# Spreading the modulation steps of a hybrid GLA/Fourier diffusion layer: one per half unit, two at a head's middle output; a load on another queue

## The chip, the cores and the metric

The kernel runs on one core of a Trainium2 chip. The metric is the device time of one execution in microseconds (us). A core has five engines, each with its own instruction stream: TensorE (PE, matmuls; its weight loads are shown as PEld), VectorE (DVE), ScalarE (ACT), GpSimd (POOL) and SyncE (SP), which in this kernel only issues transfers (DMAs). ACT and POOL issue a few DMAs too. PE, DVE, ACT and POOL run in an order that the kernel's code gives; for SP's DMAs a scheduler chooses the order.

## The reference

One layer of a diffusion backbone on 128 context and 256 latent tokens, model width 2048, everything in float32. Cut to what matters here:

```python
def layer(x, cond, s0_f, s0_b, n_chunks, lw):
    mod = jax.nn.silu(cond) @ lw['w_ada'] + lw['b_ada']
    sh1, sc1, ga1, sh2, sc2, ga2 = [m[:, None, :] for m in jnp.split(mod, N_MOD, axis=-1)]
    h = rmsnorm(x, lw['norm_pre_mix']) * (1.0 + sc1) + sh1
    m, s_f, s_b = mixer(h, s0_f, s0_b, n_chunks, lw)
    x = x + ga1 * rmsnorm(m, lw['norm_post_mix'])
    h = rmsnorm(x, lw['norm_pre_ffn']) * (1.0 + sc2) + sh2
    ff = (jax.nn.silu(h @ lw['w_ffn_gate']) * (h @ lw['w_ffn_up'])) @ lw['w_ffn_down']
    return x + ga2 * rmsnorm(ff, lw['norm_post_ffn']), s_f, s_b

def mixer(h, s0_f, s0_b, n_chunks, lw):
    # h @ w_in: GLA q, k (4 heads x 128), v, output gate g (4 x 256), two decay factors (16 each),
    # Fourier groups (4 x 256)
    # branch A: gated linear attention in both directions, chunks of 64, RMSNorm per head, times silu(g)
    # branch B: real part of the 2-D DFT over positions and group channels
    gates = jax.nn.sigmoid(h @ lw['w_gate'] + lw['b_gate'])
    g_a, g_b = jnp.split(gates, 2, axis=-1)
    merged = g_a * (o @ lw['w_br_gla']) + g_b * (f @ lw['w_br_four'])
    return merged @ lw['w_out'], s_f, s_b
```

The modulation `cond @ w_ada` has two rows only (context and latent), but its weights are 2048 x 12288.

## The kernel before, in words

**Products.** Every matrix product is done in split float32: weights and inputs each have a high and a low part, and three matmuls (high-high, high-low, low-high) stand for one. A weight block of 128 x 1024 (512 KB) takes this path: SP loads it into `raw` (two buffers, and in some stages spare ones), ACT casts the high part `whi` (`split`; L301, or L292 and L295 for folded blocks), DVE subtracts the low part `wlo` (L288), PE multiplies (L327 in `gemm`). Four pairs `whi`/`wlo` exist; `push` splits one block each time a product takes one.

**Half units.** The stages until the output projection are made of units. `proj` does a unit of 128 output columns as two half units of 24 matmuls each; after each it calls `step(side)`, which lets side work go on by one step. Side work is written as Python generators, so a `yield` is the place where the work is cut, and the order of the instructions on each engine is that in which the generators are run.

**Stages in order.** Input norm and the v projection (to 142 us); the stage of GLA, with units for q and k and the gates 0 to 24, beside which `gla()` computes the four heads (to 442 us); the gates 25 to 31, beside which `run_after` prepares the Fourier branch (`ends`, `over_parts`: sums and differences of rows, L727 to L741; `across_n`: products L1040 and L1041 with weights that `fold_across` folds, L257 and L258; to 548 us); the units of GLA's output gate, o0 to o7, with `four` units between them (products L1240 and L1241; their weights are folded by L244 and L245, cast by L295; to 663 us); the branch-a units; `w_out`; and the feed-forward net, which takes the rest.

**The modulation.** The last four of the six vectors are computed beside all this. `ada_rest` goes through blocks; each has 16 granules. A granule loads 512 KB of `w_ada` from POOL's queue into `adaw` (two buffers). On DVE it multiplies and adds this into `adacc` (two instructions L708, one for each row; L706 for the first granule of a block). With `on_pe` set it goes to TensorE instead: four products L698, which are eight rows in a trace, into `pr`. After the granules come one empty step, then the row sums (L719, products with `selr`) and ACT's copy `adev` (L668), then in the next step two transposes L672 and DVE's L677. `ada` is `ada_gen` behind `paced`, which runs `rate[0]` steps for each call on average.

**GLA.** For each head: transposes and decay (`la`, ACT L819 to L821; split into `lah` and `lal`, L379 and L380), then for both directions the sums along the chunk (`bT`, L835), `qi` and `ki` (L851, L852), the scores (`at`, L875), states, and three outputs `po` (L789) for t = 0, 1, 2. A gate's unit ends with ACT's `gz` (L983) and a store of it (L984, issued by ACT). At the end DVE scales all outputs with the norms `rs` (L946).

**The end of GLA.** `low_later` makes `split` hold back the low part of a block until the next `split`, so that DVE does other work before it.

**The constants** `cd` for the Fourier branch (128 x 1934, L1063) are loaded in `run_after`, at its turn 7 of 14.

Of the kernel before, what the change touches and what calls it, by code (L numbers as in the profile page):

```python
# [37 lines left out]
XU = 2  # L38
GF = 25
GD = 256  # L40
TAIL = {1: True, 4: False, 5: True, 8: True, 10: False, 11: True, 14: False}
RATE = 1.07


C_TRI = 0
# [7 lines left out]
C_CE = C_SEL3 + 96  # L53
# [3 lines left out]
NC = C_CT + 2 * (HT + HL)  # L57
# [51 lines left out]
def tile_step(ctx: ExitStack, tc: tile.TileContext, a, o):  # L109
# [139 lines left out]
    low_later = [False]  # L249
# [434 lines left out]
    on_pe = [False]  # L684
# [69 lines left out]
    with ExitStack() as s:  # L754
# [25 lines left out]
        def gla():  # L780
# [10 lines left out]
            for h in range(NH):  # L791
# [34 lines left out]
                yield  # L826
                if h == 0:
                    yield
                for d in range(2):


                    bT = pss.tile([P, T], F32, tag="side", name="bT")
                    for t in range(3):
                        for j, l in enumerate((lah, lal)):
                            PE.matmul(  # L835
                                bT[:, t * P : (t + 1) * P], l[:, t, d], tri[:, d * P : (d + 1) * P],
                                start=j == 0, stop=j == 1,
                            )
                    sx = pss.tile([P, 2, P], F32, tag="side", name="sx")
                    for j, l in enumerate((lah, lal)):  # L840
                        PE.matmul(
                            sx, tri[:, (2 + d) * P : (3 + d) * P], l[:, 0 : 2 + d : 1 + d, d], start=j == 0, stop=j == 1,
                        )
                    eb = pg.tile([P, T], F32, tag=f"eb{d}", name="eb")
                    ACT.activation(eb, bT, AF.Exp)
                    ki = pg.tile([P, T], F32, tag=f"ki{d}", name="ki")
                    ACT.activation(ki, bT, AF.Exp, scale=-1.0)
                    ko = pg.tile([P, 2, P], F32, tag=f"ko{d}", name="ko")
                    ACT.activation(ko, sx, AF.Exp)
                    qi = pg.tile([P, T], F32, tag=f"qi{d}", name="qi")  # L850
                    DVE.scalar_tensor_tensor(qi, eb, DK**-0.5, qT[:, h, :], op0=ALU.mult, op1=ALU.mult)  # L851
                    DVE.tensor_mul(ki, ki, kT[:, h, :])  # L852
                    DVE.tensor_mul(ko, ko, krs[:, 0 : 2 + d : 1 + d, :])

                    last = 0 if d else CH - 1
                    tot = chunks(eb)[:, :, d, last : last + 1]
                    kc = pg.tile([P, 3, CH], F32, tag=f"kc{d}", name="kc")
                    DVE.tensor_mul(kc, chunks(ki)[:, :, d, :], tot.to_broadcast([P, 3, CH]))
                    dc = pg.tile([P, 1], F32, tag=f"dc{d}", name="dc")
                    c = 5 if d else 2  # L860
                    e0, e1 = c * CH + last, (c + 1 - 2 * d) * CH + last
                    DVE.tensor_mul(dc, eb[:, e0 : e0 + 1], eb[:, e1 : e1 + 1])
                    qin.append(qi)
                    kin.append(ki)
                    kcr.append(kc)
                    kout.append(ko)
                    dec.append((tot, dc))
                    yield
# [60 lines left out]
                for t in range(3):  # L929
                    po = pss.tile([P, DV], F32, tag="side", name="po")  # L930
                    mm3(po, [x[:, t, :] for x in ap], vh[t], True, t == 0)
                    if t:
                        for d in range(2):
                            st = (sp if t == 1 + d else S)[d]
                            mm3(po, [x[:, t, :] for x in qp[d]], [x[:, 0, :] for x in st], False, d == 1)
                    ACT.copy(on(t, h), po.rearrange("p (a b) -> p a b", a=2))
                    junk = pg.tile([P, DV], F32, tag="krs", name="junk")
                    ACT.activation(junk, po, AF.Square, accum_out=ss[:, t, h : h + 1])
                    yield
            rs = pg.tile([P, 3, 4], F32, name="rs")  # L940
            ACT.activation(rs, ss, AF.Sqrt, bias=eps_t[:, 0:1], scale=1.0 / DV)
            DVE.reciprocal(rs, rs)
# [25 lines left out]
        gl = gla()  # L968
        def side():
            while True:  # L970
                next(gl, None)
                next(ada, None)
                yield

        sd = side()
        rate[0] = RATE
        for i in qk_order[1:]:
            proj(psm, hT, keep(qk, i), sd)

# [36 lines left out]
    with ExitStack() as s:  # L1016
        more = s.enter_context(tc.tile_pool(name="more", bufs=1))
        hF = [actp.tile([P, 4, 2, T], F32R, tag=t, name="hF") for t in ("C_lo", "B_hi", "B_lo")]
        hF.append(more.tile([P, 4, 2, T], F32R, tag="hF", name="hF"))
        sums, folds = [], {}  # L1020

        def ends(n):
            t, r = (more.tile([P, 2, T], F32, tag=z, name=z) for z in ("t", "r"))
            over_ends(2 * n, t, r)
            over_parts(2 * n, r, False)
            folds[n] = r

        def across_n(h, n):
            if n == 0:
                sums[:] = [pss.tile([P, 2, hi - lo], F32, tag="side", name="pfo") for _ in range(2) for lo, hi, _ in parts]  # L1030
            w = take()
            push()
            w_of = [x.rearrange("p (g i k c) -> p i k g c", g=2, i=2, k=2) for x in w]
            for k in range(2):
                kt = 2 * n + k
                x = hF[kt // 4][:, kt % 4]
                for g in range(2):
                    for i, (lo, hi, _) in enumerate(parts):
                        p = sums[2 * g + i]
                        PE.matmul(p, w_of[0][:, i, k, g, :], x[:, :, lo:hi], start=kt == 0, stop=False)  # L1040
                        PE.matmul(p[:, 0], w_of[1][:, i, k, g, :], x[:, 0, lo:hi], start=False, stop=kt == KT - 1)  # L1041
            if n == 7:
                for g in range(2):
                    X.append(px.tile([P, T], F32, tag="yb", name="X", bufs=4))
                    for i, (lo, hi, _) in enumerate(parts):
                        p = sums[2 * g + i]
                        ACT.copy(X[-1][:, lo:hi], p[:, 1])
                        DVE.tensor_add(X[-1][:, lo:hi], X[-1][:, lo:hi], p[:, 0])

        def run_after():  # L1050
            for at, todo in enumerate(after):
                for what, *n in todo:
                    if what == "ends":
                        ends(*n)
                    elif what == "parts":
                        over_parts(2 * n[0], folds.pop(n[0]), True)
                    else:
                        if n == [1, 5]:
                            depth[0] = 2
                            spare_raws.clear()  # L1060
                        across_n(*n)
                if at == turns // 2:
                    SP.dma_start(cd, a["consts"][:, C_CE:NC])  # L1063
                if at in (turns - 4, turns - 3, turns - 1):
                    next(ada_gen, None)
                yield

        ra = run_after()
        low_later[0] = True
        for i in range(GF, 32):  # L1070
            proj(psm, hT, gate(more, i), ra)
            if i == GF:
                depth[0] = 4
                spare_raws.extend([lambda: more.tile([P, G], F32, tag="raw3", name="raw3", bufs=2)] * 2)
        catch_up()
        low_later[0] = False
        depth[0] = 0
        xq = px.tile([P, HT], F32, name="xq")
        POOL.memset(xq, 0.0)
        qb = pss.tile([P, HT], F32, tag="side", name="pfq")  # L1080
        for kb in range(0, KT, 4):
            for x_ in range(2):
                for k in range(kb, kb + 4):
                    q = 32 * (k % 4)
                    PE.matmul(
                        qb[q : q + 4, :], wq[:, k, :], hF[k // 4][:, k % 4, x_, 0:HT].bitcast(F32),
                        start=kb == 0 and x_ == 0, stop=kb == KT - 4 and x_ == 1,
                    )
        for q in range(0, P, 32):
            ACT.copy(xq[q : q + 4, :], qb[q : q + 4, :])  # L1090
# [3 lines left out]
    with ExitStack() as s:  # L1094
# [84 lines left out]

        def side():  # L1180
            while True:
                on_pe[0] = turn[0] > 5
                if turn[0] < 6 or turn[0] % 2:
                    next(ada_gen, None)
                on_pe[0] = False
                turn[0] += 1
                next(df, None)
                next(nw, None)
                yield
# [910 lines left out]
```

## Time and profile before

| what | value |
|---|---|
| median of 3 runs | 1955.28 us (1954.93 to 1955.28) |
| the profiled execution | 1954.75 us |
| its span | 1953.0 us |
| TensorE's clock granted, mean | 0.997 |
| PE busy | 1923.8 us |
| DVE busy | 1650.9 us |
| ACT busy | 915.7 us |
| POOL busy | 85.8 us |
| DMA packets | 200615, 380.52 MB |

The span is the time between the first and the last event of the profiled execution; the time of the execution itself has 1.75 us more around it. Busy times leave out waits and issuing. In a row of the timeline stand the start in us from the span's start, the duration, the engine and the line, the operation with the written tile and the ones read, the shape, how many such instructions stand together (x), and in brackets how long the engine was idle just before and what it waited for. In a row of windows stand for each engine its busy time and number of instructions, then TensorE's clock, the DMA engines' share and GB/s.

### The profile page before, as it was taken

How to read it: one execution, taken by the hardware profiler on the slowest of the kernel's cores; microseconds unless marked ns; L12 is line 12 of the kernel's file. 1: busy time of each engine (PE TensorE's matmuls, PEld its weight loads, DVE VectorE, ACT ScalarE, POOL GpSimd, SP SyncE). 2: the span in 40 equal slices, each digit the busy share in tenths (PEclk: the TensorE clock that was granted, in tenths of full speed). 3: DMA queues.
4: the chain of work that ended last, by engine and by line, in shares of the span. 5: the costliest groups of instructions: out<-in, count | busy, mean ns of one | idle time of the engine just before them, and what ended most of it. 6: DMA issues, size and time to landing. Idle time of an engine off the chain costs nothing.

```text
span 1953.0 us, 27535 instructions
## 1 busy us (share of the span) xinstructions
PE 1923.8 (99%) x10526; PEld 1692.8 (87%) x10526; DVE 1650.9 (85%) x2174; ACT 915.7 (47%) x1298; POOL 85.8 (4%) x154
## 2 busy tenths in 40 slices
PE   8999999999999999999999999999999999999997
PEld 5779999999999999999988888888888888888876
DVE  5668898989868897987789898999998999888885
ACT  4235445544455644456454444444444444444444
POOL 0001111110000000004000000000000000000001
PEclk9999999999999999999999999999999999999999
DMA  9977766766556895656254635363636263625243
GB/s 390 387 257 240 252 223 230 261 233 219 181 161 227 297 310 190 222 195 220 81 176 148 189 109 190 126 207 110 205 109 215 93 221 92 200 76 183 86 168 112
DMA packets 200615, 380.52 MB, mean 195 GB/s; under 512 B 14196, under 2 KB 126932, under 8 KB 196132
## 3 DMA queue, kind: packets, MB, share of 16 engines
q1 hardware_dynamic: 181396, 321.83, 48.7%
q0 software_dynamic: 13952, 50.39, 8.5%
q10 hardware_dynamic: 5136, 6.56, 0.9%
q8 instruction: 82, 1.34, 0.3%
q14 instruction: 49, 0.40, 0.1%
HBM read 361.94 MB, written 16.78 MB: 194 GB/s over the span
## 4 chain that ended last, share of the span: by engine, by line
PE 71%; DVE 3%; DMA 1%; ACT 1%; issue 0%; ACTq 0%; DVEq 0%; SPq 0%
PE pgu L339 30%; PE pdn L339 18%; PE pmm L327 17%; PE pf L1240 1%; PE pmm L1517 1%; PE pfo L1040 1%; PE ptr L1809 1%; PE pf L1241 1%; DMA raw<-in_w_d 0%; DMA raw<-in_w_gate 0%; PE pfo L1041 0%; DVE adacc L708 0%; DVE x1b L1961 0%; DMA raw<-in_w_in 0%; PE pr L698 0%
## 5 line engine op out<-in xcount | busy, mean ns | idle before, releaser
L327 PE MATMUL pmm<-A_hi,wlo 128*128 128x384 f32 x1072 | 360.0, 336 | 4.2 <-DVE wlo L288 4.2
L327 PE MATMUL pmm<-A_hi,whi 128*128 128x384 f32 x1072 | 362.8, 338 | 0.0
L327 PE MATMUL pmm<-A_lo,whi 128*128 128x384 f32 x1072 | 359.6, 335 | 0.0
L1664 ACT CAST whi<-u 128x1024 fp32r<-128x1024 f32 x200 | 210.6, 1053 | 281.6 <-DVE u L1648 86.2
L1664 ACT CAST whi<-raw 128x1024 fp32r<-128x1024 f32 x175 | 184.2, 1052 | 202.0 <-PE pgu L339 59.4
L1675 DVE TENSOR_TENSOR wlo<-u,whi 128x1024 fp32r<-128x1024 f32 x200 | 244.3, 1222 | 31.5 <-ACT whi L1664 17.9
L339 PE MATMUL pgu<-whi,A_hi 128*128 128x512 f32 x640 | 250.0, 391 | 0.0
L339 PE MATMUL pgu<-whi,A_lo 128*128 128x512 f32 x640 | 249.3, 389 | 0.0
L1675 DVE TENSOR_TENSOR wlo<-raw,whi 128x1024 fp32r<-128x1024 f32 x175 | 213.7, 1221 | 38.5 <-ACT whi L1664 30.8
L288 DVE TENSOR_TENSOR wlo<-raw,whi 128x1024 fp32r<-128x1024 f32 x163 | 198.3, 1220 | 25.8 <-ACT whi L301 24.4
L301 ACT CAST whi<-raw 128x1024 fp32r<-128x1024 f32 x149 | 155.9, 1050 | 120.8 <-PE pmm L327 57.2
L327 PEld LDWEIGHTS pmm<-A_hi,wlo 128*128 128x128 f32 x1072 | 202.1, 188 | 4.9 <-DVE wlo L288 4.9
L327 PEld LDWEIGHTS pmm<-A_hi,whi 128*128 128x128 f32 x1072 | 202.1, 188 | 3.4 <-issue 2.5
L708 DVE SCALAR_TENSOR_TENSOR adacc<-adaw,spad,adacc 128x1024 f32<-128x1024 f32 x162 | 200.6, 1280 | 2.4 <-DMA adaw<-in_w_ada 1.9
L327 PEld LDWEIGHTS pmm<-A_lo,whi 128*128 128x128 f32 x1072 | 202.2, 189 | 0.2
L339 PE MATMUL pdn<-whi,hid_hi 128*128 128x512 f32 x480 | 186.9, 389 | 0.0
L339 PE MATMUL pdn<-whi,hid_lo 128*128 128x512 f32 x480 | 186.8, 389 | 0.0
L339 PE MATMUL pgu<-wlo,A_hi 128*128 128x512 f32 x640 | 184.2, 389 | 0.0
L339 PEld LDWEIGHTS pgu<-whi,A_hi 128*128 128x128 f32 x640 | 120.2, 188 | 26.1 <-issue 0.8
L339 PEld LDWEIGHTS pgu<-wlo,A_hi 128*128 128x128 f32 x640 | 120.1, 188 | 25.4
L339 PEld LDWEIGHTS pgu<-whi,A_lo 128*128 128x128 f32 x640 | 120.1, 188 | 25.0
L339 PE MATMUL pgu<-whi,S 128*128 128x512 f32 x480 | 131.1, 395 | 0.0
(405 smaller groups left out, 3042.7 us busy)
## 6 DMA issues: line engine op xcount, KB each, us to landing
adaw<-in_w_ada POOLq DMA_DIRECT2D x96, 512.0 KB, 3.9
raw<-in_w_d SPq DMA_DIRECT2D x88, 512.0 KB, 3.7
slab<-in_w_ada SPq DMA_DIRECT2D x32, 1024.0 KB, 10.0
raw<-in_w_gate SPq DMA_DIRECT2D x64, 512.0 KB, 4.6
raw<-in_w_g SPq DMA_DIRECT2D x48, 512.0 KB, 3.5
raw<-in_w_u SPq DMA_DIRECT2D x48, 512.0 KB, 3.6
raw<-in_w_in SPq DMA_DIRECT2D x44, 512.0 KB, 4.2
u<-in_w_u SPq DMA_DIRECT2D x40, 512.0 KB, 4.7
```

Source lines behind the costliest of these rows:

```text
L288: eng.tensor_sub(lo, raw, hi.bitcast(F32))
L301: ACT.copy(hi, raw)
L327: PE.matmul(dst, w[wi][:, k * n + n0 : k * n + n0 + P], x[xi][:, k0 + k, :], start=first and k == 0 and j == 0, stop=last and k == kts - 1 ...
L339: PE.matmul(dst, stat[x_][m], mov(w[w_], m), start=first and w_ == m == x_ == 0, stop=last and w_ == m == 1,)
L708: DVE.scalar_tensor_tensor(acc[:, c, :], w, spad[:, k, c : c + 1], acc[:, c, :], op0=ALU.mult, op1=ALU.add,)
L1040: PE.matmul(p, w_of[0][:, i, k, g, :], x[:, :, lo:hi], start=kt == 0, stop=False)
L1240: PE.matmul(pf[:, 0 : 2 * HT], w[0][:, c], x[k], start=k == 0, stop=False)
L1241: PE.matmul(pf[:, 0:HT], w[1][:, c], x[k][:, 0:HT], start=False, stop=m == 1 and k == 3)
L1517: PE.matmul(hp[u], hw[u][j][:, ((k - 1) % 8) * P : ((k - 1) % 8 + 1) * P], h2[m][:, k - 1, :], start=k == 1 and j == m == 0, stop=k == KT ...
L1664: ACT.copy(hi, src)
L1675: DVE.tensor_sub(lo, src, hi.bitcast(F32))
L1809: PE.transpose(pt[:, j, :], src[:, j * P : (j + 1) * P], ident)
```

## The change

Six edits, all but one of the order:

1. `TAIL` names the branch-a units that do a modulation granule, `True` for TensorE. It had 1, 5, 8 and 11 on TensorE, and 4, 10 and 14 on DVE; it has 8 on TensorE, and 4, 10, 13 and 15 on DVE.
2. In the GLA stage `side` drives `ada_gen` itself: once in each half unit, and twice in the one of a head's middle output (`yield t == 1`). The pace of 1.07 steps for each half unit goes.
3. Head 0 has one more `yield` between its decay and the sums along the chunk.
4. `cd` is loaded from ACT's queue and not from SP's.
5. `low_later` is set after the first of the gate units 25 to 31 and not ahead of it.
6. In the o units the half units 0 to 6 and 8 have their granule on DVE, and 7, 9, 11, 13 and 15 on TensorE; before, DVE had 0 to 5 and TensorE 7, 9, 11, 13 and 15.

```diff
-TAIL = {1: True, 4: False, 5: True, 8: True, 10: False, 11: True, 14: False}
-RATE = 1.07
+TAIL = {4: False, 8: True, 10: False, 13: False, 15: False}
...
                 split_act(lah, lal, la)
                 yield
                 if h == 0:
+                    yield
                     yield
                 for d in range(2):
...
                     ACT.activation(junk, po, AF.Square, accum_out=ss[:, t, h : h + 1])
-                    yield
+                    yield t == 1
...
         gl = gla()
         def side():
             while True:
-                next(gl, None)
-                next(ada, None)
+                light = next(gl, None)
+                for _ in range(2 if light else 1):
+                    next(ada_gen, None)
                 yield
 
         sd = side()
-        rate[0] = RATE
...
                 if at == turns // 2:
-                    SP.dma_start(cd, a["consts"][:, C_CE:NC])
+                    ACT.dma_start(cd, a["consts"][:, C_CE:NC])
...
         ra = run_after()
-        low_later[0] = True
         for i in range(GF, 32):
             proj(psm, hT, gate(more, i), ra)
             if i == GF:
                 depth[0] = 4
+                low_later[0] = True
...
         def side():
             while True:
-                on_pe[0] = turn[0] > 5
-                if turn[0] < 6 or turn[0] % 2:
+                on_pe[0] = turn[0] > 6 and turn[0] != 8
+                if turn[0] < 9 or turn[0] % 2:
                     next(ada_gen, None)
```

In the rows that follow, lines of the changed kernel are one lower than those of the same code before, up to about L826.

DVE's order at the first `four` unit inside o3, before and after. `ws` is the folded Fourier weight block, `adacc` and `adaw` are the modulation's sums and weights, `fd` takes the product.

```order
L244 TENSOR_TENSOR ws<-raw_5909 128x512
L245 TENSOR_TENSOR ws<-raw_5909 128x512
L288 TENSOR_TENSOR wlo<-ws,whi 128x1024
L288 TENSOR_TENSOR wlo<-raw_5911,whi 128x1024
L1245 TENSOR_TENSOR fd<-fd,pf 128x194 x2
```

After the change, the same place:

```order
L243 TENSOR_TENSOR ws<-raw_5909 128x512
L244 TENSOR_TENSOR ws<-raw_5909 128x512
L707 SCALAR_TENSOR_TENSOR adacc<-adaw,spad,adacc 128x1024 x2
L287 TENSOR_TENSOR wlo<-ws,whi 128x1024
L287 TENSOR_TENSOR wlo<-raw_5911,whi 128x1024
L1245 TENSOR_TENSOR fd<-fd,pf 128x194 x2
```

A granule has come between the fold and the low part; the same happens in o4.

DVE's order where the GLA stage ends and `run_after` begins, before. `qk` holds the heads' outputs, `rs` their norms; `t`, `r` and `hF` are the sums of rows; `raw` is a weight block as loaded.

```order
L946 TENSOR_SCALAR qk<-qk,rs 128x2x128 x4
L727 TENSOR_TENSOR t<-A_hi,A_lo 128x768
L732 TENSOR_TENSOR r<-t 128x2x64
L733 TENSOR_TENSOR r<-t 128x2x63
L732 TENSOR_TENSOR r<-t 128x2x128
L733 TENSOR_TENSOR r<-t 128x2x127
L257 TENSOR_TENSOR raw<-raw 128x2x256
L258 SCALAR_TENSOR_TENSOR raw<-raw 128x2x256
L288 TENSOR_TENSOR wlo<-raw,whi 128x1024
L739 TENSOR_TENSOR hF<-r,hF 128x2x384
```

After the change, the same place:

```order
L946 TENSOR_SCALAR qk<-qk,rs 128x2x128 x8
L287 TENSOR_TENSOR wlo<-raw,whi 128x1024
L726 TENSOR_TENSOR t<-A_hi,A_lo 128x768
L731 TENSOR_TENSOR r<-t 128x2x64
L732 TENSOR_TENSOR r<-t 128x2x63
L731 TENSOR_TENSOR r<-t 128x2x128
L732 TENSOR_TENSOR r<-t 128x2x127
L256 TENSOR_TENSOR raw<-raw 128x2x256
L257 SCALAR_TENSOR_TENSOR raw<-raw 128x2x256
L738 TENSOR_TENSOR hF<-r,hF 128x2x384
```

The low part has moved from behind the fold (L257 and L258 before) to ahead of the sums of rows; eight scalings stand in a row where there were four.

PE's order in gate unit 2, before, at head 0's middle output (`po`; `pr` takes the row sums, `ptm` their transposes).

```order
L789 MATMUL po<-vr,ap 128x256 x3
L789 MATMUL po<-part,qp 128x256 x6
L719 MATMUL pr<-adacc,selr 32x256 x8
L327 MATMUL pmm<-A_hi,whi 128x384
```

After the change, at the same output, which comes one half unit later:

```order
L788 MATMUL po<-vr,ap 128x256 x3
L788 MATMUL po<-part,qp 128x256 x6
L718 MATMUL pr<-adacc,selr 32x256 x8
L671 MATMUL ptm<-ident,adev 128x128 x2
L326 MATMUL pmm<-A_hi,whi 128x384
```

The transposes, which stood a half unit behind the row sums, now follow them at once.

SP's order at the end of the GLA stage, before.

```order
L235 DMA raw_4617<-in_w_in 128x4x256
L235 DMA raw_4619<-in_w_gate 128x1024
L1063 DMA cd<-in_consts 128x1934
L235 DMA raw<-in_w_gate 128x1024
```

After the change:

```order
L234 DMA raw_4617<-in_w_in 128x4x256
L234 DMA raw<-in_w_gate 128x1024
L234 DMA raw_4619<-in_w_gate 128x1024
```

The load into the ordinary buffer now comes ahead of the one into the spare buffer, and `cd` is gone from SP; ACT issues it right behind the L740 of `run_after`'s turn 7.

## The prediction, made before the change was run

> **What bounds the kernel now.** I read the busy times and the chain that ended last first, then the list of what TensorE (PE) waited for.
>
> ```profile
> PE 1923.8 (99%) x10526; PEld 1692.8 (87%) x10526; DVE 1650.9 (85%) x2174; ACT 915.7 (47%) x1298; POOL 85.8 (4%) x154
> PE 71%; DVE 3%; DMA 1%; ACT 1%; issue 0%; ACTq 0%; DVEq 0%; SPq 0%
> PE pmm L327 <- DVE wlo L288: 4.2, 2, 3.7
> PE at L875 <- DVE ki L852: 1.8, 1, 1.8
> PE pr L719 <- DVE adacc L708: 1.5, 2, 0.9
> PE bT L835 <- DVE lal L380: 0.9, 2, 0.6
> ```
>
> The first row is busy us, share of the span and instructions; the second the chain by engine; the others what PE waited for: total us, how often, the longest. PE is busy 99% of the span, so an edit pays in two ways only: it takes work off PE, or removes one of PE's few waits. It costs where a VectorE (DVE) step comes late for PE. The four waits listed lie in the stages that the diff touches: 8.4 us in all.
>
> **Granules taken off TensorE.** By the order of instructions three fewer modulation granules (not four) are on PE: those of branch-a units 1, 5 and 11. Their price is seen at the one that PE ran at 689 us (start, duration, what):
>
> ```profile
> 688.85 0.33 PE L327 MATMUL pmm<-o_lo,whi 128*128 128x384 f32 x1
> 689.02 0.34 PE L327 MATMUL pmm<-o_hi,wlo 128*128 128x384 f32 x1
> 689.29 0.64 PE L698 MATMUL pr<-adaw,spad 128*32 128x256 f32 x8
> 689.86 0.45 PE L327 MATMUL pmm<-o_hi,whi 128*128 128x384 f32 x1
> ```
>
> From one product matmul to the next it is 689.02 − 688.85 = 0.17 us; across the granule 0.84. So a granule costs PE 0.67 us, and three cost **−2.0**. The list shows no PE wait in the branch-a units, so this comes off the end. The three come back on DVE: one in the branch-a units, two in the o units.
>
> **Two granules more on VectorE in the o units.** The order puts them at the first half unit of o3 and of o4, between the fold of the Fourier weights (L245) and their low part (L288), for which the product L1241 on PE waits.
>
> ```profile
> L708 DVE SCALAR_TENSOR_TENSOR adacc<-adaw,spad,adacc 128x1024 f32<-128x1024 f32 x162 | 200.6, 1280 | 2.4 <-DMA adaw<-in_w_ada 1.9
> 601.23 1.23 DVE L288 TENSOR_TENSOR wlo<-ws,whi 128x1024 fp32r<-128x1024 f32 x1 [1.12 <-ACT whi L295]
> 607.83 0.56 DVE L380 TENSOR_TENSOR o_lo<-gs,o_hi 128x384 fp32r<-128x384 f32 x1 [0.58 <-ACT o_hi L379]
> 608.78 1.22 DVE L288 TENSOR_TENSOR wlo<-ws,whi 128x1024 fp32r<-128x1024 f32 x1 [0.39 <-ACT whi L295]
> 603.64 0.25 PE L1241 MATMUL pf<-edT,wlo 128*128 128x194 f32 x1
> 610.23 0.25 PE L1241 MATMUL pf<-edT,wlo 128*128 128x194 f32 x1
> ```
>
> The low part that ends at 602.46 is used at 603.64: 1.18 to spare. The next ends at 610.00 and is used at 610.23: 0.23 to spare. A granule is two instructions of the first row; a pair takes 2.48 (row of 185.02 below), and 187.41 − 185.02 = 2.39 until the next instruction starts. In its place DVE now idles 1.12 for an ACT cast, so each new granule delays DVE by 1.27 net. The idles of 0.58 and 0.39 don't win that back: both end on ACT casts that follow on DVE's own work. Two delays less the 0.23 to spare make 2.3; I take **+2.2**, a little less for what ACT may catch up. Bounds: 2 × 2.39 = 4.8 if the idle isn't used, 0.5 if most of the delay is taken up by later idles. I stay near the middle, as it rests on rows of the very place.
>
> The one DVE granule more in the branch-a units I put at nothing: the weights there come through the same L288, on which PE doesn't wait in that stage; without that cover it would cost 2.4.
>
> **Start of the gate units 25 to 31.** Here lies PE's longest wait in these stages.
>
> ```profile
> raw<-in_w_gate SPq DMA_DIRECT2D x64, 512.0 KB, 4.6
> 443.99 1.06 ACT L301 CAST whi<-raw 128x1024 fp32r<-128x1024 f32 x1 [0.45 <-DVE wlo L288]
> 448.31 0.96 DVE L727 TENSOR_TENSOR t<-A_hi,A_lo 128x768 f32<-128x768 f32 x1
> 449.32 1.57 SPq L1063 DMA_DIRECT2D cd<-in_consts  x1
> 451.71 1.22 DVE L288 TENSOR_TENSOR wlo<-raw,whi 128x1024 fp32r<-128x1024 f32 x1
> 453.00 0.33 SPq L235 DMA_DIRECT2D raw<-in_w_gate  x1
> 452.00:456.50 4.50, 4.50 (x28) 4.50 (x27) 4.47 (x8) 1.69 (x3) 1.31 (x3) 1.00 1.02 344
> 455.95 0.84 ACT L741 CAST hF<-r 128x768 fp32r<-128x768 f32 x1 [1.00 <-DVE r L733]
> 460.68 1.05 ACT L301 CAST whi<-raw 128x1024 fp32r<-128x1024 f32 x1 [3.89 <-DMA raw<-in_w_gate]
> 462.84 0.43 DVE L732 TENSOR_TENSOR r<-t 128x256 f32<-128x256 f32 x1 [3.57 <-ACT r L728]
> 464.84 1.22 DVE L288 TENSOR_TENSOR wlo<-raw,whi 128x1024 fp32r<-128x1024 f32 x1
> 466.12 0.69 PE L327 MATMUL pmm<-A_hi,wlo 128*128 128x384 f32 x1 [3.71 <-DVE wlo L288]
> ```
>
> Read backwards: PE waits 3.71 us at 466.12 for the low part that DVE starts at 464.84; DVE had idled 3.57 for a copy on ACT that stands behind the cast of 460.68; ACT had idled 3.89 before that cast for a w_gate load that landed at about 460.6. That load was issued at 453.00, when the low part of 451.71 had let go of its buffer (452.93), and it went out behind the load of `cd`: the last figures of the window's row are TensorE's clock (1.00), the share in which the 16 DMA engines were busy (1.02, full) and GB/s.
>
> After the change the low part that frees the buffer isn't held back behind the next split. Its cast is done at 445.05, DVE comes to it at 448.31 in place of L727, so the buffer is free at about 449.5; and in SP's order this load now stands ahead of the next w_gate load, with no `cd` before it. Issued 3.5 us earlier, with the 4.6 us of the first row, it is there at about 454.1. ACT is done with L741 at 456.79, so the cast starts there: 3.89 earlier. From the cast on the chain is as before (464.84 + 1.22 − 460.68 = 5.38), so the low part ends near 462.2, and PE needs it at 466.12 − 3.71 = 462.41. I take **−3.4**, the wait less 0.3 for small lateness on that chain. Bounds: −1.0, if the load takes its 7.6 us (453.00 to 460.6) at the new place too and meets some more delay behind it, and −3.7.
>
> The load of `cd` goes out from ACT at about 499 us, behind L741 of that step, where these rows stand:
>
> ```profile
> 494.20 0.33 SPq L235 DMA_DIRECT2D raw<-in_w_gate  x1
> 502.73 1.05 ACT L301 CAST whi<-raw 128x1024 fp32r<-128x1024 f32 x1 [2.06 <-PE pmm L327]
> ```
>
> Its issue took 1.57 us on SP. On ACT a copy of the fold and two casts are queued behind it, but ACT idles 2.06 us there, for PE and not for a load, so I put it at nothing, and at 1.57 if that idle were gone. The w_gate load of 494.20 is cast 8.5 us after its issue, so a few us of shared bandwidth cost nothing either.
>
> [...]
>
> **The GLA steps.** Modulation now takes one step in each half unit and two at a head's middle output; the total of steps is as before. From head 0's decay on, every GLA step comes one half unit later.
>
> ```profile
> 185.02 2.48 DVE L708 SCALAR_TENSOR_TENSOR adacc<-adaw,spad,adacc 128x1024 f32<-128x1024 f32 x2
> 187.41 1.22 DVE L288 TENSOR_TENSOR wlo<-raw,whi 128x1024 fp32r<-128x1024 f32 x1
> 188.55 0.55 DVE L851 SCALAR_TENSOR_TENSOR qi<-eb,qk 128x384 f32<-128x384 f32 x1
> 189.72 0.47 PE L875 MATMUL at<-qi,ki 128*64 128x64 f32 x9 [1.76 <-DVE ki L852]
> 223.98 0.64 PE L719 MATMUL pr<-adacc,selr 128*32 128x256 f32 x8 [0.91 <-DVE adacc L708]
> 225.18 0.64 PE L719 MATMUL pr<-adacc,selr 128*32 128x256 f32 x8 [0.56 <-DVE adacc L708]
> 225.88 0.37 ACT L668 COPY adev<-pr 128x256 f32<-128x256 f32 x1 [2.03 <-PE pr L719]
> 309.23 0.58 ACT L983 ACTIVATE gz<-pmm,bgate 128x384 f32<-128x384 f32 x1
> 310.21 0.87 ACT L819 ACTIVATE la<-z 128x512 f32<-128x512 f32 x2 [0.40 <-ACT gz L983]
> ```
>
> - Head 0's scores (L875) wait 1.76 for DVE, which is late by a granule and a low part. These take 188.55 − 185.02 = 3.53 us; a half unit on PE has 24 matmuls, at 0.17 each 4.1 or more. One half unit more ahead of this step lets DVE catch up about 0.6: **−0.6** (0 to −1.8).
> - The row sums of a modulation block (L719) wait 0.91 + 0.56 = 1.47 for the block's last granule, which belongs to the half unit before and which DVE comes to late. They move one half unit on, so that goes; but the two transposes then follow them at once and wait for ACT's copy, which ends at 226.25, 0.43 after the row sums do at 225.82, with some 0.15 until PE goes on: +0.6. Net **−0.9** (−1.5 to +0.5).
> - The waits for `lal` (0.9 in two heads) follow on a decay chain on ACT that stands behind a gate's evacuation: 310.21 − 309.23 = 0.98 us. With the steps moved by a half unit, the gate no longer comes in that one: **−0.9** (0 to −0.9).
> - A doubled half unit gives DVE 2 × 2.39 + 1.14 = 5.9 us of work for 4.2 us of PE. In a head's middle and last output PE needs from DVE only low parts, and the list has two waits for these in the whole run, so I put the 1.7 us of lateness at nothing; uncovered it would cost 1.7 at each of up to four places.
>
> **Sum.** −2.0 + 2.2 − 3.4 − 0.6 − 0.9 − 0.9 = −5.6 us. The profiled execution took 1954.75 us (its span 1953.0), so it would take 1949.15; the median of the runs shown is 0.53 above it: **1949.7**. A measurement of this kernel can tell about 0.2%, 3.9 us, from no change, so under 1951.4 is faster and over 1959.2 slower.
>
> **The rivals.**
>
> *The start of the gate units gains nothing.* [...] Then 3.4 is lost: 1953.1, no change. For it: the share of 1.02. Against it: `cd` is the largest transfer in the window, and the load of 494.20 has us to spare. Chance 0.18.
>
> *The o units hide their granules.* Then 2.2 less: 1947.5. For it: the 1.12 of idle, the 1.18 to spare. Against it: the 0.23. Chance 0.10.
>
> *VectorE becomes late all through the GLA heads* (the other side). The half unit put in ahead of head 0's scores also moves heads 1 to 3 against the weights' splits. If each of their scores then meets the backlog that head 0 shows, in both directions, that is 6 × 1.76 = 10.6 us: 1960.3, slower. It decides where DVE's work ahead of a head's `ki` is more than the half unit's 4.2 us. For it: DVE's 85% and the doubles. Against it: a granule and a low part are 3.53, and the list shows this wait once in four heads. Chance 0.09.
>
> That the diff doesn't do what it says is true in one point, three granules for four; the fourth would be another 0.67, and the sum has it right.
>
> **How the numbers follow.** The forecast's own case has 0.63. Its unknown sizes reach from −3.7 for the start, 0.5 for the o units and −4.2 for the three GLA terms (−9.4 in all, not likely together) to −1.0, 4.8 and 0.5, which with −2.0 is +2.3. About five sixths of it lies under 1951.4, with nearly all of the second rival: 0.63. The first rival and the rest of the forecast's case make no change: 0.29. The third and a tail make 0.08. The range goes from 1946.5 (the o units hidden and the start's whole 3.7, and some more) to 1955.0 (the first rival, with 2 us for the upper part of the o units).
>
> **What would show it.** In the changed kernel: no wait near 3.7 at the first gate unit after the `hF` product, and the w_gate load ahead of it issued by 450 and cast by 457; at the first `four` units after o3 and o4 small waits of L1241 for L288, 2 us together; three `L698` groups fewer; no wait of L719 for L708, but one of the transposes L672 for ACT's copy; the wait at L875 near 1.1. I am wrong if the start's wait is still over 2 us, if waits for L288 in the o units come to over 4, or if L875 waits in several heads.

## The result: 0.996 of the time before

The changed kernel took 1947.15 us (median of 5 runs, 1946.11 to 1947.94) beside 1954.93 before; the ratio is 0.9960, with a 95% interval of 0.9946 to 0.9975. The forecast was 1949.7. Its profiled execution took 1947.15 us (span 1945.3), 7.6 less than that of before. Each experiment below was measured beside fresh runs of the kernel before, whose medians went from 1954.75 to 1955.62; so kernels are compared here by their ratios, and two ratios that differ by less than their intervals reach to one side, some 0.0012, are not told apart.

The busy times and the waits of PE in the changed kernel, in the form of those shown of before:

```profile
PE 1918.5 (99%) x10502; PEld 1689.6 (87%) x10502; DVE 1656.2 (85%) x2180; ACT 915.5 (47%) x1298; POOL 85.8 (4%) x154
PE pf L1241 <- DVE wlo L287: 2.0, 3, 0.7
PE pmm L326 <- DVE wlo L287: 1.9, 1, 1.9
PE at L875 <- DVE ki L852: 1.4, 1, 1.4
PE ptm L671 <- ACT adev L667: 0.5, 1, 0.5
PE bT L835 <- DVE lal L379: 0.4, 1, 0.4
L707 DVE SCALAR_TENSOR_TENSOR adacc<-adaw,spad,adacc 128x1024 f32<-128x1024 f32 x168 | 208.0, 1279 | 8.3 <-DMA adaw<-in_w_ada 8.0
```

Of the kernel before, the wait of the Fourier products:

```profile
PE pf L1241 <- DVE wlo L288: 0.7, 1, 0.7
```

Among the waits in the stages that the diff touches one is new, that of the transposes (0.5), and one has grown, that of the Fourier products in the o units (2.0 where there was 0.7). The row sums' wait is gone, and the one for low parts of gate units is less than half. The last of the changed kernel's rows is DVE's: it waits 8.0 us for modulation weights, 1.9 before.

The start of the gate units, in the changed kernel (SP, ACT, DVE, PE):

```profile
448.64 0.81 SPq L234 DMA_DIRECT2D raw<-in_w_gate  x2
455.77 1.05 ACT L300 CAST whi<-raw 128x1024 fp32r<-128x1024 f32 x1
460.26 1.22 DVE L287 TENSOR_TENSOR wlo<-raw,whi 128x1024 fp32r<-128x1024 f32 x1
461.53 0.45 PE L326 MATMUL pmm<-A_hi,wlo 128*128 128x384 f32 x1 [1.94 <-DVE wlo L287]
461.81 0.34 PE L326 MATMUL pmm<-A_hi,whi 128*128 128x384 f32 x1
461.99 0.33 PE L326 MATMUL pmm<-A_lo,whi 128*128 128x384 f32 x1
```

The load is issued at 448.64 and not at 453.00, ACT casts at 455.77 and not at 460.68, and the low part is there at 461.48. Neither the cast nor the low part has idle time in brackets: no load is waited for here any more. The low part starts 3.4 us after its cast ends, since DVE works without a gap on the sums of rows and the fold ahead of it. PE waits 1.94.

The matmuls behind the same wait in the kernel before, with the windows around it (the last three figures are TensorE's clock, the DMA share and GB/s):

```profile
466.60 0.52 PE L327 MATMUL pmm<-A_hi,whi 128*128 128x384 f32 x1
466.92 0.52 PE L327 MATMUL pmm<-A_lo,whi 128*128 128x384 f32 x1
465.00:466.10 1.10, 0.00 (x0) 0.00 (x0) 1.10 (x2) 1.08 (x2) 0.00 (x0) 0.50 0.00 0
468.00:470.00 2.00, 2.00 (x8) 2.00 (x7) 1.97 (x6) 0.20 (x1) 0.00 (x0) 0.50 0.74 234
472.00:474.00 2.00, 2.00 (x15) 2.00 (x14) 2.00 (x3) 1.55 (x3) 0.00 (x0) 1.00 0.17 12
```

Here is what the forecast did not have. After its 3.71 us of waiting PE ran at half its clock: matmuls 0.32 us apart, not 0.17, from 466.1 to about 472. After the 1.94 us of the changed kernel they are 0.18 apart at once.

How much earlier or later the same matmul starts than in the profile of before (us, worked out from the traces, at matmuls near these places of before's time):

| kernel | 441, end of GLA | 473, behind the start of the gate units | 590, first o units | 667, last o unit | 735, branch-a | 1200, feed-forward |
|---|---|---|---|---|---|---|
| changed | −2.6 | −7.2 | −7.8 | −5.5 | −7.8 | −7.8 |
| changed, again (e12_after) | +0.7 | −3.5 | −4.1 | −1.9 | −4.3 | −4.3 |
| e1_start | −0.7 | −6.7 | −6.1 | −6.1 | −6.1 | −6.1 |
| e2_gla | −1.1 | +0.7 | −0.1 | −0.1 | −0.1 | −0.1 |
| e4_o_tail | −0.9 | +0.3 | +0.2 | +2.4 | +0.1 | +0.1 |
| e5_cd_only | −1.0 | −3.5 | −2.6 | −2.6 | −2.6 | −2.7 |
| e6_low_only | +0.4 | −5.0 | −5.1 | −5.1 | −5.1 | −5.1 |
| e7_o_back | +2.4 | −2.2 | −2.9 | −3.0 | −4.4 | −4.5 |
| e8_skip | −4.4 | −11.1 | −11.7 | −9.5 | −11.8 | −11.9 |
| e9_best | −3.1 | −9.8 | −10.5 | −10.5 | −12.8 | −12.8 |
| e10_no_yield | +0.1 | −6.4 | −5.7 | −3.5 | −5.8 | −5.8 |
| e11_no_double | +1.8 | −1.4 | −1.5 | +0.7 | −1.6 | −1.6 |

Differences between neighbouring columns are what a stage brought. The first column has noise: the five kernels whose GLA stage is as before (e1, e3, e4, e5, e6) range there from −1.0 to +0.7. (e3 is not in the table, since its 20 extra matmuls shift the count.)

### The profile page after: what moved, and what is told of

It reads as the page before. It is cut to its first block, busy times and chain, and to the rows that moved or that the text cites. A ratio compares the mean times of both kernels' runs of the same rounds, so it can differ in the third digit from the quotient of the medians.

```text
span 1945.3 us, 27489 instructions
## 1 busy us (share of the span) xinstructions
PE 1918.5 (99%) x10502; PEld 1689.6 (87%) x10502; DVE 1656.2 (85%) x2180; ACT 915.5 (47%) x1298; POOL 85.8 (4%) x154
## 4 chain that ended last, share of the span: by engine, by line
PE 85%; DVE 8%; DMA 3%; ACT 2%; issue 2%; SPq 0%; DVEq 0%; ACTq 0%
PE pgu L338 30%; PE pmm L326 24%; PE pdn L338 18%; PE pv L491 3%; DVE adacc L707 3%; DVE wlo L287 1%; PE pgm L474 1%; PE pfo L1040 1%; PE pmm L1517 1%; PE pf L1240 1%; DMA adaw<-in_w_ada 1%; DMA slab<-in_w_ada 1%; PE ptr L1809 1%; PE pfo L1041 1%; DMA xraw<-in_w_x 0%
## 5 line engine op out<-in xcount | busy, mean ns | idle before, releaser
L707 DVE SCALAR_TENSOR_TENSOR adacc<-adaw,spad,adacc 128x1024 f32<-128x1024 f32 x168 | 208.0, 1279 | 8.3 <-DMA adaw<-in_w_ada 8.0
```

Of the source, the lines that this page charges most:

```text
L707: DVE.scalar_tensor_tensor(acc[:, c, :], w, spad[:, k, c : c + 1], acc[:, c, :], op0=ALU.mult, op1=ALU.add,)
```

## The experiments

The theory to test (A): the gain comes from the start of the gate units, where a wait costs itself and then half a clock; the GLA terms are taken back there; and the granules of edits 1 and 6 cancel. The rival (B): the forecast's terms, which add.

**e1_start: edits 4 and 5 alone.**

```diff
-                    SP.dma_start(cd, a["consts"][:, C_CE:NC])
+                    ACT.dma_start(cd, a["consts"][:, C_CE:NC])
...
-        low_later[0] = True
         for i in range(GF, 32):
...
                 depth[0] = 4
+                low_later[0] = True
```

> Edits 4 and 5 alone (cd from ACT, low_later after the first unit) on the kernel before. Theory A (a long wait costs twice: the wait of 3.71 us, and then TensorE at half clock for about 6 us, some 2.6 us more): PE comes to the first gate unit's low part as early as before (462.4 us), the low part is there by 461.5 to 462.2, so the wait is under 0.5 and the clock stays at 1.00: 3.4 + 2.6 = 6.0 us faster, 1948.9. Rival B (the forecast's: only the wait counts): 3.4 faster, 1951.5, with the slow matmuls behind it still there.

Measured: 1948.39 us, ratio 0.9963 (0.9951 to 0.9975). PE at the place:

```profile
462.05 0.44 PE L327 MATMUL pmm<-A_hi,wlo 128*128 128x384 f32 x1 [0.52 <-DVE wlo L288]
462.33 0.34 PE L327 MATMUL pmm<-A_hi,whi 128*128 128x384 f32 x1
```

The wait is 0.52 and the clock 1.00 (461 to 464): A. By the ratios (0.9963 and 0.9960) these two edits alone bring what the whole change brings.

**e2_gla: edits 2 and 3 alone**, on the kernel before.

> Edits 2 and 3 alone (one modulation step in each half unit, two at a middle output; one more yield for head 0). Theory A (the start of the gate units is set by the load behind cd, then by DVE, not by when PE gets there): PE leaves the GLA stage 2.5 us earlier, and the wait at the gate units' start grows from 3.7 to about 6, with the half clock behind it as before; 0 to 0.5 faster, about 1954.6. Rival B (the forecast's terms simply add): 2.5 faster, 1952.4, the wait stays 3.7.

Measured: 1953.48 us, ratio 0.9992 (0.9983 to 1.0001). PE at the start of the gate units:

```profile
463.36 0.44 PE L327 MATMUL pmm<-A_hi,whi 128*128 128x384 f32 x1 [2.59 <-ACT whi L301]
467.69 0.69 PE L327 MATMUL pmm<-A_hi,wlo 128*128 128x384 f32 x1 [3.71 <-DVE wlo L288]
468.18 0.52 PE L327 MATMUL pmm<-A_hi,whi 128*128 128x384 f32 x1
```

PE came 1.1 us earlier and was 0.7 later behind the start: it waits in two pieces, 6.3 us in all, with the half clock behind (0.50 from 466 to 470). In the profile that is A's; the ratio, 1.6 us faster with no change inside its interval, lies between the two.

**e3_warm: extra matmuls in the wait.**

```diff
+    fill = [0]
...
         p = pool.tile([P, T], F32, tag="mm", name="pmm")
+        for _ in range(fill[0]):
+            PE.matmul(p, x[0][:, 0, 0:P], x[0][:, 0, :], start=True, stop=True)
...
         for i in range(GF, 32):
+            fill[0] = 20 if i == 27 else 0
             proj(psm, hT, gate(more, i), ra)
+            fill[0] = 0
```

> The kernel before, with 20 extra matmuls (128x128 by 128x384, results overwritten) on PE ahead of gate unit 27's first product, where PE otherwise waits 3.71 us. They leave the low part as late as it is. Theory A (the half clock comes from PE's idle time): PE is idle under 1 us there, the clock stays at 1.00, matmuls behind it are 0.17 us apart: 2.6 us faster, 1952.3, with 20 matmuls more. Rival B (the slow matmuls come from something else at that place, such as transfers or weight loads): they stay 0.32 us apart and the time is that of before, 1954.9.

Measured: 1951.93 us, ratio 0.9984 (0.9973 to 0.9995), by which it is 3.1 us faster with 20 matmuls more. PE, and a window behind it:

```profile
462.34 3.68 PE L355 MATMUL pmm<-A_hi 128*128 128x384 f32 x20
469.24 0.44 PE L327 MATMUL pmm<-A_hi,wlo 128*128 128x384 f32 x1 [2.87 <-DVE wlo L288]
469.52 0.34 PE L327 MATMUL pmm<-A_hi,whi 128*128 128x384 f32 x1
469.30:471.00 1.70, 1.70 (x10) 1.70 (x11) 1.70 (x2) 0.84 (x1) 0.00 (x0) 1.00 0.45 96
```

In this profile the low part came 3.1 us later than in that of before (its load was issued at 454.82 and not at 453.00, and cast at 463.81 and not at 460.68), so PE still waits 2.87, more than expected. But the clock stays at 1.00, and the feed-forward net begins when it did although the low part came 3.1 later: the full clock is worth some 3 us. The transfers and weight loads of the place are still there, so B falls. Here 2.87 us of waiting are left and don't halve the clock, where 2.42 in e5 and 1.77 in e11 did; so it is not the length of a wait alone that decides, and the last section comes back to it.

**e4_o_tail: edits 1 and 6 alone**, on the kernel before.

> Edits 1 and 6 alone (three granules off TensorE in the branch-a units, two of them onto DVE in the o units). Theory A (as the traces of before and after read): -2.35 for the three granules, +2.25 for the two low parts that come late in the o units; together nothing, 1954.8. Rival B (the o units hide the granules): 2.3 faster, 1952.6.

Measured: 1954.96 us, ratio 0.9997 (0.9989 to 1.0006). In the table it loses 2.3 us between 590 and 667 and gains 2.3 between 667 and 735: A. The two edits pay for each other. (The wait at the start of the gate units, whose code is that of before, is in this profile 1.5 and then 3.7, as in e2.)

**e5_cd_only and e6_low_only: edits 4 and 5 each alone.**

> Edit 4 alone (cd from ACT's queue at turn 7) on the kernel before. The w_gate load is still issued at 453 us but with no cd ahead of it. Theory A (the 3.7 us wait came from this load standing behind cd, and cost the half clock too): it lands near 457.7 and not 460.6, the low part is there at about 463.1, the wait is about 0.7 and the clock stays 1.00: 3.0 + 2.6 = 5.6 us faster, 1949.3. Rival B (full DMA engines delay it wherever cd is, so the transfer only moves): the wait stays over 2.5, and the time falls by under 1.5.

> Edit 5 alone (low_later only after the first of the gate units 25 to 31) on the kernel before; cd stays on SP, now behind two w_gate loads. Theory A: the load that PE's wait hangs on is issued ahead of cd and about 3.5 us earlier; wait under 0.7, clock 1.00, 6.0 us faster, 1948.9, so that edits 4 and 5 bring about the same, each alone, and little more together. Rival B (each brings its share, they add): about half of what both brought, 3 us faster, 1951.9.

Measured: with `cd` moved 1952.45 us, ratio 0.9986 (0.9977 to 0.9995); with the low part moved 1949.06 us, ratio 0.9966 (0.9953 to 0.9978). PE in the first and then in the second:

```profile
463.66 0.69 PE L327 MATMUL pmm<-A_hi,wlo 128*128 128x384 f32 x1 [2.42 <-DVE wlo L288]
464.14 0.52 PE L327 MATMUL pmm<-A_hi,whi 128*128 128x384 f32 x1
464.46 0.52 PE L327 MATMUL pmm<-A_lo,whi 128*128 128x384 f32 x1
```

```profile
463.67 0.44 PE L327 MATMUL pmm<-A_hi,wlo 128*128 128x384 f32 x1 [1.08 <-DVE wlo L288]
463.95 0.34 PE L327 MATMUL pmm<-A_hi,whi 128*128 128x384 f32 x1
```

Edit 5, one line, brings about all that edits 4 and 5 bring together: that is A. Edit 4 alone lies between the two theories: its time fell by 2.7 us by the ratio, where A had 5.6 and B under 1.5. It leaves a wait of 2.42, and that still halves the clock (0.50 from 464 to 466); A's 0.7 was too low: in this profile PE needed the low part 1.2 us earlier than reckoned and got it 0.5 later.

**e7_o_back: the o units as before, the branch-a granules all on DVE.**

```diff
-TAIL = {4: False, 8: True, 10: False, 13: False, 15: False}
+TAIL = {1: False, 4: False, 5: False, 8: False, 10: False, 13: False, 15: False}
...
-                on_pe[0] = turn[0] > 6 and turn[0] != 8
-                if turn[0] < 9 or turn[0] % 2:
+                on_pe[0] = turn[0] > 5
+                if turn[0] < 6 or turn[0] % 2:
```

> The changed kernel, with the o units as before (DVE granules at half units 0 to 5, TensorE at 7, 9, 11, 13, 15) and all seven granules of the branch-a units on DVE (units 1, 4, 5, 8, 10, 13, 15). Theory A (two low parts in the o units come late by these granules; the branch-a units have 8 to 9 us to spare): 2.25 us back in the o units, 0.67 for one granule less on TensorE, so 2.9 faster than the changed kernel, near 1944.3 where before has 1954.9. Rival B (DVE has no room left in the branch-a units): four granules of 2.39 more there make waits for L288, and it is no faster than the changed kernel.

Measured: 1947.41 us (1942.96 to 1950.92), ratio 0.9962 (0.9948 to 0.9976): as the changed kernel, which is B's time. PE in the branch-a units:

```profile
695.55 0.36 PE L1241 MATMUL pf<-edT,wlo 128*128 128x194 f32 x1 [1.37 <-DVE wlo L287]
```

The o units lose nothing (590 to 667), but units 4 and 5, both on DVE now, make a wait of 1.37. So in this profile A is right for the o units and B for the branch-a units. Besides, the GLA stage, whose code is the changed kernel's, ended 5.0 later in it (the table's first column); from there on it gains more than the changed kernel does.

**e8_skip: no modulation step in the last GLA half unit** (`quiet` is set ahead of it), one more at turn 9 of `run_after`.

```diff
-                for _ in range(2 if light else 1):
+                for _ in range(0 if quiet[0] else 2 if light else 1):
                     next(ada_gen, None)
...
-                if at in (turns - 4, turns - 3, turns - 1):
+                if at in (turns - 5, turns - 4, turns - 3, turns - 1):
```

> The changed kernel, with the modulation step of the last GLA half unit (gate unit 24) left to a later half unit (turn 9 of the gate units 25 to 31); all work is still done. Theory A (the 1.94 us that PE still waits at gate unit 27 is DVE's backlog, one granule of 2.39 ahead of it): the wait is under 0.3, 1.8 us faster than the changed kernel, near 1945.3 where before has 1954.9. Rival B (what is left is the load or ACT): the wait stays above 1.3 and the time is that of the changed kernel.

Measured: 1945.82 us, ratio 0.9954 (0.9941 to 0.9966). PE at the start of the gate units no longer waits; the first matmul with a low part there:

```profile
457.69 0.34 PE L326 MATMUL pmm<-A_hi,wlo 128*128 128x384 f32 x1
458.22 0.34 PE L326 MATMUL pmm<-A_hi,wlo 128*128 128x384 f32 x1
```

One granule less ahead of it on DVE, and the 1.94 us are gone: A. By time alone e8 and the changed kernel are hardly told apart (0.9954 beside 0.9960 and 0.9966); the rows show it.

**e10_no_yield and e11_no_double: the changed kernel without edit 3, and without edit 2.**

> The changed kernel without edit 3 (head 0's extra yield); the steps are still one per half unit and two at a middle output. Theory A: the scores' wait of head 0 comes back (about 1.6 us where the kernels with edit 3 have 0.7), the waits for lal (0.9) and for the row sums (1.5 for 0.5) too, so PE leaves GLA 2.8 us later; 1.9 of that is taken back, since the wait at the gate units' start is set by DVE and goes: 0.9 slower than the changed kernel. Rival B (the terms add): 2.8 slower, and the start still waits 1.9.

> The changed kernel without edit 2 (pace of 1.07 steps as before; edit 3 stays). Theory A: the row sums stand a half unit earlier again and wait 1.0 us more in all, and the start of the gate units takes that back: the changed kernel's time within 0.5. Rival B (the double at a middle output is what brings the gain in GLA): over 1.5 slower.

Measured: 1948.62 us, ratio 0.9968 (0.9956 to 0.9980), without the yield; 1952.38 us, ratio 0.9990 (0.9981 to 1.0000), without the doubles. In the first PE leaves GLA 2.7 later than in the first profile of the changed kernel, and only 0.8 of it is left behind the start, where PE no longer waits: A. In the second A is wrong, and the time is B's (over 1.5 slower). The row sums there, and a window:

```profile
223.97 0.91 PE L719 MATMUL pr<-adacc,selr 128*32 128x256 f32 x8 [2.74 <-DVE adacc L708]
224.00:227.00 3.00, 2.80 (x19) 1.24 (x20) 2.15 (x2) 1.52 (x5) 0.96 (x2) 0.53 0.87 259
465.74 0.45 PE L327 MATMUL pmm<-A_hi,wlo 128*128 128x384 f32 x1 [1.77 <-DVE wlo L288]
466.00:468.00 2.00, 2.00 (x9) 2.00 (x9) 2.00 (x3) 0.63 (x1) 0.00 (x0) 0.64 0.59 143
```

The wait of 2.74 for the block's last granule halves the clock (0.53 in the window), and so does the 1.77 at the start (0.64 in a window that holds the drop, 0.51 from 468 to 470). So with edit 3 in place edit 2 is needed (0.9990 without it). Edit 3 itself brings nothing that the times show: without it the ratio is 0.9968, with it 0.9960 and 0.9966.

**e12_after: the changed kernel once more.**

> The changed kernel once more, beside the others on one chip. Theory A: 0.996 of before; the wait at the gate units' start is near 1.9 and the clock there 1.00; DVE's wait for adaw near 380 us, 0.5 in the first profile, 2.9 and 1.9 in e2 and e7 and none in e8, differs from run to run, and where it is over 1.5 PE waits behind it. Rival B: the wait near 380 is a property of each kernel's order, and is 0.5 again.

Measured: 1947.36 us (1946.64 to 1950.31), ratio 0.9966 (0.9954 to 0.9978). Its profiled execution was the slowest, 1950.31 us. DVE and PE near 385 us in it, and a window:

```profile
380.92 1.28 DVE L707 SCALAR_TENSOR_TENSOR adacc<-adaw,spad,adacc 128x1024 f32<-128x1024 f32 x1 [2.44 <-DMA adaw<-in_w_ada]
386.43 0.33 PE L835 MATMUL bT<-cg,lah 128*128 128x128 f32 x1 [2.02 <-ACT lah L378]
390.00:392.00 2.00, 2.00 (x7) 2.00 (x7) 1.82 (x6) 1.84 (x4) 0.00 (x0) 0.50 0.62 223
```

The first profile had 0.48 at the same place and no such wait on PE. So it is not fixed by the order (A): with edits 2 and 3 a granule near 380 us can find its weights not landed, head 3's decay stands behind it on DVE, PE waits for that, and the clock halves behind it (0.50 from 390 to 392). This is most of the 3.2 us between the two profiled executions. In e2 and e7 DVE waited 2.9 and 1.9 there, in e8 and e9 not; none of the kernels without edit 3 did. Why the load is late there stays open.

**e9_best: the three improvements together** (e8's step, the o units as before, `TAIL` with 1, 4, 8, 10, 13 and 15 on DVE and 5 on TensorE).

> The changed kernel, with the step left out of the last GLA half unit as in e8_skip, the o units as before the change, and branch-a granules on DVE at units 1, 4, 8, 10, 13, 15 and on TensorE at unit 5 only (not 4 and 5 both on DVE, behind which PE waited 1.37 us in e7_o_back). Theory A: e8's time less the 2.25 us of the o units: 1943.5 where before has 1955. Rival B (two DVE granules more in the branch-a units still make a wait of 1 us or more there): 1944.7.

Measured: 1942.09 us (1941.03 to 1946.99), ratio 0.9940 (0.9925 to 0.9954). PE has no wait for a low part in the gate units, and one of 0.7 in the Fourier products; 590 to 735 brings 2.3 us, where the changed kernel had nothing. A; by the medians it is 5 us below the changed kernel. B's 1944.7 lies inside the interval too; the rows speak against it, since no wait of 1 us is left in the branch-a units.

## Why the prediction was right

The sum came out (−5.6 forecast, −7.6 in the profiles, −7.8 in the medians), but partly by luck: the half clock, about 2.7 us (an estimate: 18 matmuls 0.32 us apart and not 0.17), wasn't in it, and the GLA terms, −2.4, were in it but are mostly taken back. Point by point:

- **Granules off TensorE:** −2.0 forecast, −2.3 from 667 to 735 in the changed kernel and in e4. Right; three granules, as counted.
- **Granules in the o units:** +2.2 forecast, +2.25 from 590 to 667, +2.3 in e4. Right, by the mechanism given: a low part behind a granule, with 0.2 us to spare. PE waits twice for it, 0.69 each time, and goes on 1.1 later each time. The rival that they are hidden falls.
- **Start of the gate units:** −3.4 forecast with −3.7 as the bound, −4.6 measured, by two errors that partly cancel. The step that failed is "the low part ends near 462.2, and PE needs it at 462.41". The low part ended at 461.48, better than that; but PE, which the GLA terms had brought there 2.8 earlier, needed it at 459.59. So 1.94 of the wait was left. And the term had no entry for the half clock, which cost about 2.7 more before (1.8 of the 4.6 is the wait). In e1, without the GLA edits, the step holds: a wait of 0.52.
- **The GLA terms:** −2.4 forecast, −2.6 at the end of GLA in the first profile. That this agrees is luck too: the six profiles with edits 2 and 3 range there from −4.4 to +2.4. And the terms can't be added: e1, without them, has the ratio 0.9963 where the changed kernel has 0.9960 and 0.9966. Most of what they bring is taken back at the next place that DVE sets, as e2 and e10 show. The row sums' wait went as forecast; the one for `lal` went only in part (0.9 before, 0.4 and 0.7 in the changed kernel). The transposes' new wait (0.5 for 0.6) came as forecast. The scores' wait can't be read from one profile: it was 0.9 to 2.2 in seven profiles without edit 3 among these, before's 1.76 among them, and 0 to 1.4 in those with it.
- **A small one not forecast:** before waits 0.53 at 532.34 for a low part (the second of two in the row of waits), and the changed kernel doesn't: −0.7. DVE's fold ahead of it waits 2.31 for a load in before and 1.62 in the changed kernel. PE's wait was 0 to 1.4 over the runs; what decides it stays open.
- **The first rival** (the start of the gate units gains nothing) falls for the changed kernel, by the 4.6 measured there. ACT issued the transfer at 486.5 us, not at 499 as forecast:

```profile
486.52 0.37 ACTq L1063 DMA_DIRECT2D cd<-in_consts  x1
```

From there until 588 us PE waits for nothing in the changed kernel. In e6 `cd` still comes from SP, behind the load that mattered, and the gain is the same as with edit 4 on top (0.9966 and 0.9963). What counted is which load goes first. In e5 the transfer not only changes its queue but also goes out 39 us later (488.6, not 449.3); no run tells the two apart.

- **The rival on the other side** (VectorE late in all heads) falls: no score waits but head 0's.

What the change as a whole comes to: edit 5 brings about what all six do; 1 and 6 cancel; 2 and 3 bring nothing that the ratios show, and make the end of GLA vary more from profile to profile (−4.4 to +2.4, where it was −1.0 to +0.7).

## What to carry to other kernels

A gain ahead of a place that another engine sets is not a gain: before adding terms, ask for each later wait whether what is waited for moves along. Behind a PE wait like the 1.77 us that halved the clock in e11, read the granted clock in narrow windows; here half a clock cost about 2.7 us, by estimate, behind a wait of 3.71. And where a buffer's release decides the next load's place in the queue, look for the instruction that holds the buffer before moving transfers to other queues.

## What the runs showed of the hardware

Not expected: in the kernel before, TensorE's clock was half (0.50) from 464.94 to 471.76 us, at and behind a wait of 3.71 us. The length of a wait alone doesn't decide: 1.77 us halved the clock in e11, and 2.87 left it at 1.00 in e3.

| kernel, place | PE's wait, us | clock behind it (where it was read, us) |
|---|---|---|
| before, gate units | 3.71 | 0.50 (466.1 to 468) |
| e11_no_double, row sums | 2.74 | 0.53 (224 to 227) |
| e5_cd_only, gate units | 2.42 | 0.50 (464 to 465) |
| e11_no_double, gate units | 1.77 | 1.00 (465 to 466), then 0.64 (466 to 468) and 0.51 (468 to 470) |
| e12_after, near 387 us | 2.02 and 0.67 | 1.00 (386 to 388), then 0.77 (388 to 390) and 0.50 (390 to 392) |
| e2_gla, near 387 us | 2.62 in all | 1.00 (380 to 390 and 390 to 400) |
| e3_warm, gate units | 2.87 | 1.00 (469.3 to 471) |
| changed, gate units | 1.94 | 1.00 (461.5 to 464) |
| e12_after, gate units | 2.3 | 1.00 (465.2 to 468) |

Nor does the drop always come at the same point of a wait: in before it lies inside it, 2.53 us after PE had stopped at 462.41, and at e11's gate units it comes 0.8 us after PE had gone on at 465.74 (the matmul of 466.37 takes 0.36 us, the one of 466.54 takes 0.50). The waits rest on matmul ends that the profile models, so they are rough. What decides whether and when the clock halves stays open.
